# Normed, transposed and split input rows kept in DRAM between two projections of a hybrid encoder layer

## The chip, the cores and the metric

The kernel runs on one core of a Trainium2 chip. The metric is device time in microseconds for one execution of the whole program, both request batches included. The core has five engines with a queue each: PE (TensorE, matrix products), DVE (VectorE), ACT (ScalarE), POOL (GpSimd) and SP (SyncE, which here issues most of the transfers). Each engine works through its queue in order and waits on semaphores. Transfers issued from SP, ACT or POOL are carried out by 16 DMA engines.

## The reference

One encoder layer is applied to two inputs with the same weights: a sample of 2048 tokens and a prompt of 512, both 1024 wide. All is float32.

```python
h = rms_norm(x, norm1_g)
p = h @ w_in                                  # 1024 -> 1792 columns
q, k, v = p[..., :512], p[..., 512:640], p[..., 640:768]
pool_in, hy_in = p[..., 768:1024], p[..., 1024:]
a = windowed_attention(q, k, v, ...)          # blocks of 128, QK norm, ALiBi, sink
b = multiscale_pool(pool_in, ...)
c = hyena_mixer(hy_in, ..., filters, ...)     # FFT convolutions, two orders
cat = concat(rms_norm(a), rms_norm(b), rms_norm(c))
x = x + cat @ w_out
h = rms_norm(x, norm2_g)
u = dwconv3(h @ w_ffn_in)                     # 1024 -> 2 * 2816 columns
x = x + (gelu(u[..., :2816]) * u[..., 2816:]) @ w_ffn_out
```

## The kernel before, in words

**Products.** A float32 product is made of three faster ones: each operand is split into a high part, which is a rounded copy written by ScalarE, and a low part, the difference, written by VectorE. `mm3` (L326, L327, L328) issues high x high, high x low and low x high into one PSUM bank. So each operand lives on the chip as a pair, twice its size.

**Input rows.** For a block of 128 tokens ("a row" below) `norm_load` (L338) loads 512 KB into the tile `nx`, which has two buffers. `norm` squares and sums it (ACT, L346), forms the mean (DVE, L347) and the inverse root (POOL, L349, tile `rr`) and scales it (DVE, L350). `norm_t` then transposes it in eight pieces of 128x128 on PE (L360), four to a bank, and splits each bank into the tile `h`: high part by ACT (L363), low part by DVE (L364). The result of a row is 128 partitions x 2 parts x 8 pieces x 128 tokens, 1 MB.

**The front.** `front` makes the first projection of both inputs. The combined matrix is too large to stay in SBUF as split pairs, so the columns are taken in two passes over the rows of the sample, and two over the prompt. The list `rows` holds this order: 16 rows of the sample for the columns of pooling and hyena (kind `p`, result transposed, `project_p`, stored to `pT`), then 16 rows of the sample and 4 of the prompt for query, key and value (kind `q`, `project_qkv`, stored to `qkv`), then the 4 rows of the prompt for the columns of kind `p`. Before the change each of these 40 entries goes through `norm_load`, `norm` and `norm_t`. Rows of kind `p` come in pairs into tiles `h0` and `h1` of 256 tokens; rows of kind `q` alternate between two halves of one tile `h0`. Weight blocks of 256 columns are loaded as `raw` (four loads of 256 KB, two buffers) and split into `W0` to `W3` (ACT L320, DVE L321). After the projections `front` makes the output product of the sample (L1240, stored to `x2`), which needs the attention.

**What sets the order.** `front` is the main generator, and a second chain (`side` in `run`) does the filter spectra, pooling, hyena, attention, and the start of the feed-forward part. `drive` steps one and the other by counts of nominal cost. `feed` is a background generator of `front`: it prepares row `i` as soon as `blocked(i)` allows, that is when the buffer's last reader has been issued; `xs` holds two normed rows ahead, with a nominal time before which their transposes are not issued. From these steps a scheduling layer forms a static order for every engine, so a change of the steps also changes where other work stands.

**The queues around the change.** SP issues, among others, `nx`, `raw`, the spectra's loads `dec` (L721) and `tf` (L755), the hyena's loads, and the stores of the projections (`pTs` L488, `qkvs` L511). POOL issues the stores of `x2` (L651) and computes `rr`, pooling sums and the key and query norms of the attention (`hr` L1016, `kn` L1057, `qn` L1062).

Of the kernel before, what the change touches and what calls it, by code (L numbers as in the profile page):

```python
# [11 lines left out]
F32 = mybir.dt.float32  # L12
# [7 lines left out]
KD = DM // 128  # L20
# [12 lines left out]
class Seq:  # L33


    def __init__(self, name, L):
        self.name = name
        self.L = L
        self.N2 = 2 * L // 64
        self.J = self.N2 // 2  # L40
        self.R = self.N2 // 4
        self.G = 32 // self.J
        self.Cp = 256 // self.G
        self.NC = self.Cp // 64
        self.NB = L // 128
# [197 lines left out]
class Trunk:  # L243
    def __init__(self, ctx, tc, d):
        self.ctx, self.tc, self.nc, self.d = ctx, tc, tc.nc, d
        self.dr = ctx.enter_context(tc.tile_pool(name="dr", bufs=1, space=DRAM, reuse_waits="tile"))
        self.qkv, self.pT, self.kd, self.cat, self.x2, self.act = {}, {}, {}, {}, {}, {}
        for s in SEQS.values():
            n = s.name
            self.qkv[n] = self.dr.tile([s.L, 768], F32, name="qkv" + n)  # L250
            self.pT[n] = self.dr.tile([DM, s.L], F32, name="pT" + n)
            self.kd[n] = self.dr.tile([2, 128, 32, s.Cp], F32, name="kd" + n)
            self.cat[n] = self.dr.tile([DM, s.L], F32, name="cat" + n)
            self.x2[n] = self.dr.tile([s.L, DM], F32, name="x2" + n)
            self.act[n] = self.dr.tile([D_FF, s.L], F32, name="act" + n)
        self.ops = [self.dr.tile([128, 7, 4, FH], F32, name=f"ops{i}") for i in range(2)]
# [111 lines left out]
    def front(self):  # L368


        nc, tc, d = self.nc, self.tc, self.d
        S, P = SEQS["s"], SEQS["p"]
        rows = [("p", "s", t) for t in range(S.NB)] + [("q", s.name, t) for s in (S, P) for t in range(s.NB)]
        rows += [("p", "p", t) for t in range(P.NB)]
        NS, NQ, NT = S.NB, P.NB + S.NB, len(rows)
        with tc.tile_pool(name="front", bufs=1, reuse_waits="tile") as pool:
            two = ExitStack()

# [3 lines left out]
            st = {"chunks": 0, "rows": 0, "n": 0, "pace": PACE}  # L382
            widen()
            H, ready, xs, pend = {}, set(), [], []

            def load(i):
                _, n, t = rows[i]
                return self.norm_load(pool, d["x_" + n][0, t * 128:t * 128 + 128, :], 128, NXB)

            def wide(tag, here):  # L390
                return (pool if here else st["more"]).tile([128, 2, KD * 256], F32R, tag=tag, name=tag)
# [22 lines left out]
            def step():  # L414
                if pend and next(pend[0], -1) == -1:
                    pend.pop(0)

            def finish(g):
                while g in pend:
                    step()  # L420

            def norm(i, x):
                xs.append((self.norm(pool, g1, x, 128), self.now + T_NORM))

            def place(i):

                kind, n, t = rows[i]
                if kind == "p":
                    j = (i if n == "s" else i - NQ) // 2
                    if i % 2 == 0:  # L430
                        b = j % 2 if n == "s" else (j + 1) % 2
                        H[j] = wide(f"h{b}", b == 0).rearrange("p a (k f) -> p a k f", k=KD)
                    return H[j][:, 0], H[j][:, 1], i % 2 * 128
                if i == NS:
                    t = wide("h0", True)
                    st["hq"] = [t[:, i].rearrange("p (a k t) -> p a k t", a=2, k=KD) for i in range(2)]
                v = st["hq"][i % 2]
                return v[:, 0], v[:, 1], 0

            def blocked(i):  # L440
                kind, n, _ = rows[i]
                if kind == "q":
                    return st["chunks"] < NS // 2 - 1 or st["rows"] < i - NS - 1
                if n == "s":
                    return st["chunks"] < i // 2 - 1
                return "wide" not in st if (i - NQ) // 2 == NS // 2 else st["rows"] < NQ

            def feed():
                for i in range(2, NT):
                    while blocked(i):  # L450
                        yield None
                    x, t = xs.pop(0)
                    yield from self.until(t)
                    yield from self.norm_t(x, 128, *place(i), gt)
                    if i + 2 < NT:
                        norm(i + 2, load(i + 2))
                    ready.add(i)

            def also(it):

# [65 lines left out]
            norm(1, x0[1])  # L526
            for i in range(2):
                step()
                for _ in self.norm_t(xs.pop(0)[0], 128, *place(i), self.rotate((0, 1, 2))):
                    pass  # L530
                ready.add(i)
            finish(wp[0][1])
            self.strict = False
            for i in range(2, 4):
                norm(i, load(i))
            g, gt = self.rotate((0, 1)), self.rotate((2,))
            bg = feed()
            wq = []
            for j in range(NS // 2):
# [58 lines left out]
            for m in (3, 0, 1, 2):  # L598
                w, f = wp[m]
                finish(f)  # L600
                for j in js:
                    i = NQ + 2 * j
# [11 lines left out]
            t = wide("h0", True)  # L614
# [26 lines left out]
            for t in range(S.NB):  # L641
                hi, lo, sq, x, at = box.pop(0)
                yield from self.until(at)
                r = self.out_scale(pool, g, sq, GROUPS)
# [1040 lines left out]
```

## Time and profile before

| | us |
|---|---|
| median of 3 runs | 3129.38 |
| lowest, highest | 3128.49, 3129.58 |
| the profiled execution | 3122.65 |
| its span, first to last instruction | 3120.9 |

| engine | busy us | share of the span | instructions |
|---|---|---|---|
| PE | 2968.3 | 95% | 15464 |
| DVE | 1935.9 | 62% | 3138 |
| ACT | 1318.6 | 42% | 2229 |
| POOL | 595.9 | 19% | 446 |

The DMA engines moved 399.28 MB, 128 GB/s over the span. The mean granted clock of TensorE was 0.987.

How to read it: a row of instructions names the line, the engine, the operation, the tile written, an arrow and what is read, without buffer numbers; then the shape and the count, the busy time, the mean duration of one in ns, and the idle time of the engine just before these instructions with what ended most of it. A row of waits reads "who <- for whom: us in total, times, longest". PEld is the load of the stationary operand, which overlaps PE. "SPq" or "ACTq" is the queue of an engine, where transfers are issued. Since matmuls overlap in the array, a busy PE does not mean that it is at its peak.

### The profile page before, as it was taken

Reading aid. Unit: us, or ns where it says so; the run is one execution under the profiler, and the core shown is the slowest. Engines: PE = TensorE matmul, PEld = TensorE weight load, DVE = VectorE, ACT = ScalarE, POOL = GpSimd, SP = SyncE. Lnnn points to the kernel's source line nnn. Section 1 sums busy time; section 2 is a strip of 40 time slices with the busy share of each in tenths; the row PEclk is TensorE's granted clock in tenths of the full one; section 3 lists DMA queues with packets and bytes.
Section 4 is the critical chain, followed back from the end, with each engine's and each line's share of the span. In section 5 each row is a group of like instructions: output and inputs, shape, how many; then the busy total and the mean of one; then the engine's idle time right before and its main releaser. Section 6 shows DMA issues by size and latency. Waiting matters only on the chain.

```text
span 3120.9 us, 41156 instructions
## 1 busy us (share of the span) xinstructions
PE 2968.3 (95%) x15464; PEld 2464.6 (79%) x15464; DVE 1935.9 (62%) x3138; ACT 1318.6 (42%) x2229; POOL 595.9 (19%) x446
## 2 busy tenths in 40 slices
PE   7999999999999989999869999989999999999999
PEld 6887898888878867787658888868888778888887
DVE  7443567759998768766568888877777642111111
ACT  5222454448876547644344444444444431111110
POOL 1000000012333232002144444433323200000000
PEclk9999999999999999999989999989999999999999
DMA  5555586663533446576642222232222254222222
GB/s 178 146 151 143 165 233 167 188 174 99 154 97 97 145 159 200 144 201 201 215 160 70 81 81 81 81 128 82 82 81 82 76 168 134 75 81 95 75 74 75
DMA packets 433036, 399.28 MB, mean 128 GB/s; under 512 B 75641, under 2 KB 365049, under 8 KB 430021
## 3 DMA queue, kind: packets, MB, share of 16 engines
q1 hardware_dynamic: 419733, 362.14, 39.2%
q10 hardware_dynamic: 10224, 24.03, 2.0%
q0 software_dynamic: 2880, 10.49, 0.8%
q8 instruction: 122, 2.00, 0.3%
q14 instruction: 77, 0.63, 0.1%
HBM read 292.76 MB, written 103.81 MB: 127 GB/s over the span
## 4 chain that ended last, share of the span: by engine, by line
PE 44%; DMA 2%; DVE 2%; POOL 1%; issue 1%; ACT 1%; ACTq 0%; SPq 0%; POOLq 0%; DVEq 0%
PE b L326 15%; PE b L327 15%; PE b L328 15%; DMA rw<-in_w_ffn_out_dram 2%; DVE cv L1445 1%; DVE wo L321 0%; ACT wo L320 0%; POOL o L321 0%; POOL fs L1397 0%; DMA fw<-in_w_ffn_in_dram 0%; DVE cv L1450 0%; POOL fs L1399 0%; DVE o L321 0%; ACT fk L320 0%; POOL fs L1398 0%
## 5 line engine op out<-in xcount | busy, mean ns | idle before, releaser
L326 PE MATMUL b<-o,fk 128*128 128x512 f32 x1056 | 420.2, 398 | 16.9 <-ACT fk L320 13.3
L327 PE MATMUL b<-o,fk 128*128 128x512 f32 x1056 | 420.6, 398 | 5.3 <-DVE o L321 4.4
L328 PE MATMUL b<-o,fk 128*128 128x512 f32 x1056 | 420.3, 398 | 2.5 <-DVE fk L321 2.5
L326 PE MATMUL b<-wo,ah 128*128 128x512 f32 x880 | 348.9, 396 | 7.1 <-ACT wo L320 7.1
L327 PE MATMUL b<-wo,ah 128*128 128x512 f32 x880 | 348.8, 396 | 0.2 <-DVE wo L321 0.2
L328 PE MATMUL b<-wo,al 128*128 128x512 f32 x880 | 348.6, 396 | 0.1
L321 DVE TENSOR_TENSOR al<-ar,ah 128x512 fp32r<-128x512 f32 x110 | 75.9, 691 | 406.6 <-ACT ah L320 406.6
L1445 DVE SCALAR_TENSOR_TENSOR cv<-u,cst,cv 128x1024 f32<-128x1024 f32 (+2 forms) x264 | 300.7, 1180 | 7.7 <-ACT cv L1443 3.8
L320 ACT ACTIVATE ah<-ar 128x512 fp32r<-128x512 f32 x110 | 69.2, 630 | 458.1 <-PE b L327 453.1
L326 PEld LDWEIGHTS b<-o,fk 128*128 128x128 f32 x1056 | 199.9, 189 | 66.2 <-ACT fk L320 13.7
L327 PEld LDWEIGHTS b<-o,fk 128*128 128x128 f32 x1056 | 200.1, 189 | 54.5 <-DVE o L321 4.8
L328 PEld LDWEIGHTS b<-o,fk 128*128 128x128 f32 x1056 | 200.1, 189 | 52.0 <-DVE fk L321 3.7
L326 PE MATMUL b<-W,h 128*128 128x256 f32 (+1 forms) x672 | 224.7, 334 | 3.1 <-DVE x L1240 1.6
L1408 DVE TENSOR_TENSOR u<-b,u 128x512 f32<-128x512 f32 x220 | 151.2, 687 | 121.0 <-PE b L328 118.4
L327 PE MATMUL b<-W,h 128*128 128x256 f32 (+1 forms) x672 | 214.6, 319 | 0.7 <-DVE W L321 0.3
L328 PE MATMUL b<-W,h 128*128 128x256 f32 (+1 forms) x672 | 213.6, 318 | 0.0
L326 PEld LDWEIGHTS b<-wo,ah 128*128 128x128 f32 x880 | 165.5, 188 | 48.7 <-ACT wo L320 8.0
L326 PE MATMUL b<-h,W 128*128 128x256 f32 x640 | 200.6, 314 | 3.0 <-ACT W L320 1.1
L327 PEld LDWEIGHTS b<-wo,ah 128*128 128x128 f32 x880 | 165.4, 188 | 41.4 <-DVE wo L321 1.0
L328 PEld LDWEIGHTS b<-wo,al 128*128 128x128 f32 x880 | 165.5, 188 | 41.2 <-DVE al L321 0.8
L1397 POOL TENSOR_TENSOR fs<-fw 128x512 f32<-128x512 f32 x44 | 95.9, 2180 | 510.3 <-DMA fw<-in_w_ffn_in_dram 322.1
L328 PE MATMUL b<-h,W 128*128 128x256 f32 x640 | 185.3, 290 | 3.8 <-DVE W L321 3.8
(229 smaller groups left out, 6731.8 us busy)
## 6 DMA issues: line engine op xcount, KB each, us to landing
fw<-in_w_ffn_in_dram SPq DMA_DIRECT2D x132, 512.0 KB, 3.8
ar<-acts SPq DMA_DIRECT2D x88, 256.0 KB, 2.7
nx<-in_x_sample_dram SPq DMA_DIRECT2D x32, 512.0 KB, 4.5
tf<-in_t2f_s_dram SPq DMA_DIRECT2D x64, 256.0 KB, 3.2
ops<-o SPq DMA_DIRECT2D x8, 1792.0 KB, 8.7
st<-ops SPq DMA_DIRECT2D x14, 1024.0 KB, 5.4
raw<-in_w_in_dram SPq DMA_DIRECT2D x44, 256.0 KB, 3.1
acts<-cv ACTq DMA_DIRECT2D x22, 512.0 KB, 4.2
```

Source lines behind the costliest of these rows:

```text
L320: self.keep(nc.scalar.activation(hi, x, AF.Copy))
L321: self.keep((engine or nc.vector).tensor_tensor(lo, x, hi.bitcast(F32), op=ALU.subtract))
L326: nc.tensor.matmul(ps, lhsT=lhi, rhs=rhi, start=start, stop=False, skip_group_check=more)
L327: nc.tensor.matmul(ps, lhsT=lhi, rhs=rlo, start=False, stop=False, skip_group_check=more)
L328: nc.tensor.matmul(ps, lhsT=llo, rhs=rhi, start=False, stop=stop, skip_group_check=more)
L1397: nc.gpsimd.tensor_tensor(s12[:, 0:4], a21, a22, op=ALU.add)
L1408: nc.vector.tensor_tensor(o, ps, x, op=ALU.add)
L1445: nc.vector.scalar_tensor_tensor(o, u[:, part, c + i - 1:c + i - 1 + k], self.fcw[:, i, m:m + 1], o, op0=ALU.mult, op1=ALU.add)
```

## The change

Each row is normed, transposed and split once, where it is first needed. The finished pair is written to a DRAM tile `hT`, one per row of either input, and where the list comes to the row a second time, it is read back into place. `first` lists the 20 entries that are a row's first: the 16 sample rows of kind `p`, and the 4 prompt rows of kind `q`. The writes are issued on SP behind the row's split, the reads on POOL. `place` now returns one view of both parts.

```diff
@@ __init__
+            self.hT[n] = [self.dr.tile([128, 2, KD, 128], F32, name=f"hT{n}{t}") for t in range(s.NB)]
@@ front
+        first = [i for i in range(NT) if rows[i][1:] not in [r[1:] for r in rows[:i]]]
...
+            def transposed(i, x, bank):
+                v = place(i)
+                yield from self.norm_t(x, 128, v[:, 0], v[:, 1], 0, bank)
+                nc.sync.dma_start(out=self.hT[rows[i][1]][rows[i][2]], in_=v.bitcast(F32))
+                ready.add(i)
...
                 for i in range(2, NT):
                     while blocked(i):
                         yield None
+                    if i not in first:
+                        nc.gpsimd.dma_start(out=place(i), in_=self.hT[rows[i][1]][rows[i][2]])
+                        ready.add(i)
+                        continue
                     x, t = xs.pop(0)
                     yield from self.until(t)
-                    yield from self.norm_t(x, 128, *place(i), gt)
-                    if i + 2 < NT:
-                        norm(i + 2, load(i + 2))
-                    ready.add(i)
+                    yield from transposed(i, x, gt)
+                    k = first.index(i) + 2
+                    if k < len(first):
+                        norm(first[k], load(first[k]))
...
             for i in range(2):
                 step()
-                for _ in self.norm_t(xs.pop(0)[0], 128, *place(i), self.rotate((0, 1, 2))):
+                for _ in transposed(i, xs.pop(0)[0], self.rotate((0, 1, 2))):
                     pass
-                ready.add(i)
```

Over the whole program the orders differ in these counts: transposes L360 352 before, 192 after; squares L346, scalings L350 and roots L349 60 and 40 (the other 20 belong to the feed-forward part); splits L363 and L364 88 and 48 each; loads of input rows on SP 40 and 20; new are 20 writes on SP and 20 reads on POOL.

Three places. First SP at the start of the program, where the weight blocks W0 and W1 are loaded (numbers behind the names tell buffers apart). Before:

```order
L404 DMA raw_139<-in_w_in_dram 128x2x256
L338 DMA nx_163<-in_x_sample_dram 128x1024
L404 DMA raw_157<-in_w_in_dram 128x2x256
L338 DMA nx_172<-in_x_sample_dram 128x1024
L404 DMA raw_213<-in_w_in_dram 128x2x256
L721 DMA dec_636<-in_dec_s_dram 128x256
L721 DMA dec_645<-in_dec_s_dram 128x256
L755 DMA tf_883<-in_t2f_s_dram 128x512
L755 DMA tf_921<-in_t2f_s_dram 128x512
L404 DMA raw_237<-in_w_in_dram 128x2x256
```

Now (the changed file's lines: L407 is the load of `raw`, L339 that of `nx`, L445 the new write, L500 the store of `pT`):

```order
L407 DMA raw_160<-in_w_in_dram 128x2x256
L339 DMA nx_185<-in_x_sample_dram 128x1024
L445 DMA hTs0_57<-h0_144 2048x1x128
L445 DMA hTs1_58<-h0_144 2048x1x128
L407 DMA raw_179<-in_w_in_dram 128x2x256
L339 DMA nx_194<-in_x_sample_dram 128x1024
L407 DMA raw_235<-in_w_in_dram 128x2x256
L445 DMA hTs2_59<-h1_288 2048x1x128
L407 DMA raw_259<-in_w_in_dram 128x2x256
L339 DMA nx_316<-in_x_sample_dram 128x1024
L500 DMA pTs_74<-o_255 128x2x256
L407 DMA raw_263<-in_w_in_dram 128x2x256
```

The writes of rows 0 and 1 stand ahead of the fourth load of `raw`, that of row 2 ahead of the sixth, and the first loads for the spectra have moved behind the eleventh. The 128 x 2 x 8 pieces of 128 numbers (512 bytes) of a sample row are the 2048x1x128.

Second, SP later in the first projection, in the changed kernel, where the spectra's loads `dec` (L732) and `tf` (L766) and their stores `kds` (L774) pass by:

```order
L766 DMA tf_2215<-in_t2f_s_dram 128x512
L774 DMA kds_75<-ev_2024 128x4x64 x2
L445 DMA hTs10_67<-h1_2003 2048x1x128
L339 DMA nx_2051<-in_x_sample_dram 128x1024
L774 DMA kds_75<-ev_2074 128x4x64 x2
L445 DMA hTs11_68<-h1_2003 2048x1x128
L339 DMA nx_2112<-in_x_sample_dram 128x1024
L500 DMA pTs_74<-o_2142 128x2x256
L766 DMA tf_2239<-in_t2f_s_dram 128x512
```

Each write has come in between two rows of the old sequence, mostly next to the load of a later input row; the next load of `tf` stands behind it.

Third, POOL from the end of the query rows to the first attention blocks. Before:

```order
L349 TENSOR_TENSOR rr_6264<-ss_6261,mhalf_78 128x1
L349 TENSOR_TENSOR rr_6467<-ss_6464,mhalf_78 128x1
L349 TENSOR_TENSOR rr_6681<-ss_6678,mhalf_78 128x1
L1016 TENSOR_TENSOR hr_6608<-hss_6605,mhalf_78 128x5
L1057 TENSOR_TENSOR kn_6610<-kt_6598,hr_6608 128x640
```

Now (L1027, L1068 and L1073 are `hr`, `kn` and `qn`, L461 is the new read):

```order
L461 DMA h0_3131<-hTs14_71 128x2048
L461 DMA h0_3131<-hTs15_72 128x2048
L350 TENSOR_TENSOR rr_6004<-ss_6001,mhalf_98 128x1
L350 TENSOR_TENSOR rr_6248<-ss_6245,mhalf_98 128x1
L461 DMA h1_6602<-hTp0_79 128x16x128
L461 DMA h1_6602<-hTp1_80 128x16x128
L1027 TENSOR_TENSOR hr_6430<-hss_6427,mhalf_98 128x5
L1068 TENSOR_TENSOR kn_6432<-kt_6420,hr_6430 128x640
L1027 TENSOR_TENSOR hr_6439<-hss_6436,mhalf_98 128x8
L1073 TENSOR_TENSOR qn_6441<-qt_6423,hr_6439 128x1024
L461 DMA h0_7056<-hTp2_81 128x16x128
```

The sixteen reads of the sample's rows stand on POOL one behind the other (the last two are shown), where the roots `rr` stood; the prompt's four reads stand ahead of and among the attention's norms, and go to tiles of 256 tokens in pieces of 512 bytes.

More of the change, by code (lines that the diff above doesn't have):

```diff
@@ L246, in __init__ @@
         self.dr = ctx.enter_context(tc.tile_pool(name="dr", bufs=1, space=DRAM, reuse_waits="tile"))
-        self.qkv, self.pT, self.kd, self.cat, self.x2, self.act = {}, {}, {}, {}, {}, {}
+        self.qkv, self.pT, self.kd, self.cat, self.x2, self.act, self.hT = {}, {}, {}, {}, {}, {}, {}
         for s in SEQS.values():
             n = s.name
+            self.hT[n] = [self.dr.tile([128, 2, KD, 128], F32, name=f"hT{n}{t}") for t in range(s.NB)]
             self.qkv[n] = self.dr.tile([s.L, 768], F32, name="qkv" + n)
@@ L432, in place @@
                         H[j] = wide(f"h{b}", b == 0).rearrange("p a (k f) -> p a k f", k=KD)
-                    return H[j][:, 0], H[j][:, 1], i % 2 * 128
+                    return H[j][:, :, :, i % 2 * 128:i % 2 * 128 + 128]
                 if i == NS:
@@ L436, in place @@
                     st["hq"] = [t[:, i].rearrange("p (a k t) -> p a k t", a=2, k=KD) for i in range(2)]
-                v = st["hq"][i % 2]
-                return v[:, 0], v[:, 1], 0
+                return st["hq"][i % 2]
+            def transposed(i, x, bank):
[3 more added lines that the diff above has]
+                ready.add(i)
             def blocked(i):
```

## The prediction

> **What bounds the kernel now.** I read the stages first: the busy time of each engine in seven stretches (columns: stretch, its length, then busy time and instructions of PE, weight loads, DVE, ACT, POOL, the granted clock, the share of the DMA engines, GB/s).
>
> ```profile
> core 0: us, PE busy (x) PEld busy (x) DVE busy (x) ACT busy (x) POOL busy (x), PEclk, DMA share, GB/s
> 0.00:60.00 60.00, 43.38 (x249) 36.10 (x250) 40.16 (x68) 32.56 (x53) 7.57 (x12) 0.94 0.61 193
> 60.00:350.00 290.00, 280.52 (x2100) 252.31 (x2099) 134.44 (x233) 85.02 (x147) 8.77 (x16) 1.00 0.53 146
> 350.00:700.00 350.00, 325.04 (x2386) 298.64 (x2385) 235.07 (x351) 162.01 (x274) 19.39 (x22) 1.00 0.68 190
> 700.00:850.00 150.00, 138.66 (x988) 126.50 (x988) 137.71 (x374) 130.91 (x318) 46.03 (x37) 1.00 0.42 126
> 850.00:1135.00 285.00, 278.02 (x1434) 227.74 (x1433) 234.02 (x577) 173.96 (x387) 85.12 (x111) 1.00 0.37 115
> ```
>
> The first projection runs to about 350, the query rows to about 700, the prompt's second pass and the output products to 1135; spectra, hyena and attention are woven in. TensorE is busy 93 to 98% of every stretch but the start, where it works 43 of 60 us and the queues feed weights. From 700 on VectorE is nearly full too (137.71 of 150). So time leaves this kernel when PE gets fewer instructions, or waits less; VectorE's and ScalarE's savings count only through PE's waits. Nothing behind 1135 is touched, and I let it stand.
>
> A busy PE overlaps its matmuls, so I take the price of a transpose from starts, not durations. The timeline of PE around one group of four:
>
> ```profile
> 394.54 0.28 PE L326 MATMUL b<-W,h 128*128 128x256 f32 x1
> 394.66 0.28 PE L327 MATMUL b<-W,h 128*128 128x256 f32 x1
> 394.77 0.28 PE L328 MATMUL b<-W,h 128*128 128x256 f32 x1
> 394.89 0.60 PE L360 MATMUL b<-cst,nx 128*128 128x128 f32 x4
> 395.24 0.36 PE L326 MATMUL b<-W,h 128*128 128x256 f32 x1
> 395.44 0.28 PE L327 MATMUL b<-W,h 128*128 128x256 f32 x1
> ```
>
> Products follow each other every 0.12 us. From the start of the four transposes to the second product behind them 0.55 us pass, of which one product owns 0.12: four transposes displace 0.43 us.
>
> **What is removed.** Twenty of forty rows (16 query rows, 4 rows of the prompt's second pass) lose load, norm, transposes and split: 20 x 2 groups of four transposes, 40 x 0.43 = **17.2 us** of PE. The other engines, in the groups by line up to 1140 and in the waits of 350 to 700:
>
> ```profile
> L364 DVE TENSOR_TENSOR h<-b,h 128x512 fp32r<-128x512 f32 x88 | 60.0, 686 | 66.6 <-ACT h L363 66.4
> L350 DVE SCALAR_TENSOR_TENSOR nx<-nx,rr,g 128x1024 f32<-128x1024 f32 x46 | 59.3, 1288 | 23.9 <-POOL rr L349 22.6 <-DMA g<-in_norm_g_dram 1.2
> ...
> PE b L914 <- DVE zt L900: 4.7, 8, 1.2
> PE b L831 <- DVE zg L918: 3.6, 4, 1.6
> PE b L360 <- DVE h L364: 3.5, 2, 2.9
> ...
> SPq L338 <- PE b L360: 58.4, 9, 16.2
> ```
>
> PE's waits for the bank in front of a transpose go with it: **3.5 us**. VectorE loses 1.29 + 2 x 0.69 = 2.7 us a row, 43 us over the 16 query rows, 18% of its 235.07 there. The larger waits of PE for VectorE in that stretch are 4.7 and 3.6 beside a few of 1 to 2, some 13 us in all as an estimate; 18% of it is **2.5 us** (0 if they are latency, 13 if they are queueing). ScalarE loses as many instructions, without effect of its own. The last row says that SP's queue stood 58.4 us in that stretch for a buffer that the transposes free, with loads of the hyena behind it. That goes too; PE's waits for DMA there are so small that I count nothing. Gain: 17.2 + 3.5 + 2.5 = **23.2 us**.
>
> **What is added.** Twenty writes of 1 MB on SP, behind the split of each first-seen row, and twenty reads of 1 MB on POOL, against twenty loads of 512 KB that go. The nearest rows (issue, count, KB each, median us to landing):
>
> ```profile
> nx<-in_x_sample_dram SPq DMA_DIRECT2D x32, 512.0 KB, 4.5
> tf<-in_t2f_s_dram SPq DMA_DIRECT2D x64, 256.0 KB, 3.2
> ops<-o SPq DMA_DIRECT2D x8, 1792.0 KB, 8.7
> hst<-pTs SPq DMA_DIRECT2D x6, 1024.0 KB, 7.0
> x2s<-x POOLq DMA_DIRECT2D x16, 512.0 KB, 3.1
> ```
>
> `ops` is written in the same 512-byte pieces as the sample's new writes. What one write of 1 MB keeps the engines from others: at least 1.7 us for the 768 KB between `hst` and `ops`, so 2.3 for 1 MB; at most 8.7 x 1024/1792 = 5.0. In 60 to 350 a share of 0.53 moves 146 GB/s, so all engines 275, and 1 MB takes 3.8. I take 3.8, between the ends and from the stage itself.
>
> The Trainium skill, DMA: Bandwidth & Descriptors, section "Anatomy of one DMA", fits a transfer (measured on POOL's path) as about 2.0 us fixed plus bytes over 436 GB/s; by it, as an estimate, `ops` would land in 6.2 us, and the row says 8.7, so the trace does not agree for such pieces. By the page a write would occupy 2.4 us, less than the slack of 2.8 found below, and with the start at 3 the sum would be about -15 us instead of mine.
>
> *The start.* Four writes stand among the sixteen loads of the first four weight blocks. What they delay:
>
> ```profile
> 14.04 0.38 SPq L404 DMA_DIRECT2D raw<-in_w_in_dram  x1
> ...
> 14.88 0.60 ACT L363 ACTIVATE h<-b 128x512 fp32r<-128x512 f32 x1 [0.26 <-PE b L360]
> ...
> 17.80 0.61 ACT L320 ACTIVATE W<-raw 128x512 fp32r<-128x512 f32 x1
> ```
>
> The load issued at 14.04 is now behind the writes of rows 0 and 1, and the second of these waits for a split whose ScalarE half starts at 14.88. So it is issued at about 16.5 and has 2 MB ahead of it: its split comes some 7 us later than 17.80. Later blocks have two raw buffers and PE work between them, and only part comes through. I take **5 us** on PE for the whole start; ends 2 (one write's price at its lowest) and 20 (4 x 5.0).
>
> *The rest of the first projection.* Twelve writes. Behind them wait the spectra's loads, whose matmuls PE takes in order. Timelines of SP and PE:
>
> ```profile
> 196.41 0.35 SPq L755 DMA_DIRECT2D tf<-in_t2f_s_dram  x1
> ...
> 202.45 1.05 PE L758 MATMUL b<-x,tf 128*128 128x128 f32 x8
> ```
>
> From issue to use 6.0 us, landing 3.2: a slack of 2.8. A write of 3.8 ahead of such a load shows 1.0 us; between filter steps there is no such load. I take 0.4 a write, **5 us**; ends 0 and 12 x (5.0 - 2.8) = 26. The wait of a write for its split replaces a wait of the next row's load, for the transposes, at about the same place.
>
> *The query rows' reads.* POOL has nothing else in its queue there, so a waiting read holds nobody but the next. A row is 72 products of 0.12 = 8.6 us; its buffer is refilled within the row between: 7.0 landing (`hst`) and 0.6 issue leave 1 us. Later rows have hyena work between them, the first four almost none. I take **2 us**; ends 0 and 4 x (3.8 - 1.0) = 11. Over 350 to 700 the traffic grows by 8 MB, 30 us of engines at 0.68 of 350: it stays under one.
>
> The Trainium skill, same page, "Issuing engines are not separate DMA queues", says that transfers from POOL share the 16 engines with all others. The trace of before has no POOL transfer beside heavy traffic to test it on; it is why I give these reads no bandwidth of their own.
>
> *Attention.* The last reads, into two row blocks in 512-byte pieces, stand on POOL ahead of key and query norms. A POOL issue takes 0.6 us for 128 pieces:
>
> ```profile
> L651 POOL DMA_DIRECT2D x2s<-x x16: 577/610/767, 874.6 to 1136.5; - x16
> ```
>
> For 2048 pieces it lies between 0.6 and 16 times that, 39 us over four reads; POOL is busy 31% of that stretch, so at most 12 us meet waiting work. VectorE, nearly full there, loses only four rows, 11 us, so part of what PE gains earlier may queue for it. **3 us** for both; ends 0 and 12.
>
> **Sum.** -23.2 + 5 + 5 + 2 + 3 = **-8.2 us**. The profiled execution took 3122.65 (span 3120.9) and would take 3114.4; the median of the runs shown is 6.7 higher, 3129.38, and I forecast against it: **3121 us**. Every added operation hides under PE; where that cover is gone each has its upper end above.
>
> **The rivals.**
>
> *The writes pace the first projection (slower).* Each of the twelve meets the spectra's loads at the upper price: 5.0 - 2.8 = 2.2, and 0.3 for its issue, 2.5 us; 30 instead of 5 gives +16.8, **3146 us**. It decides from (23.2 - 10) / 12 = 1.1 us a write. For it: those loads run in bursts with a slack of 2.8. Against: PE's waits for them are small now, beside 512 KB row loads in the same queue. 25%.
>
> *Everything hides.* -23.2, **3106 us**: the DMA share is 0.53 and 0.68, and buffers are two deep. Against: the start, where PE already idles. 17%.
>
> *The start shows whole (no change).* Four writes at 3.8 on the weight chain, 15.2 instead of 5: +2.0, **3131 us**. For it: 43 of 60 us busy and a clock of 0.94. Against: two raw buffers. 20%.
>
> That the rows would still be made twice is excluded: the order has 192 transposes for 352.
>
> **How the numbers follow.** 38% go to the forecast, whose own range is 3114 to 3128. A run of this kernel is told from no change at about 0.2%, 6.3 us. Faster: all of "hides", four fifths of the forecast and a little of the rest, 0.49. Same: a fifth of the forecast and most of the start's rival, 0.24. Slower: the writes' rival and the start's upper part, 0.27. The range goes from 3105 to 3144: it cuts the upper part of the slower rival and any relief of VectorE beyond 2.5 us.
>
> **What would show it.** Right: 192 transposes of L360, PE's busy time down by 15 to 20 us by 1135; the waits of SP for L360 gone from the query rows; weight splits of the start 4 to 8 us later; PE's waits for `tf` grown by a few us in 60 to 350; POOL reads landing in under 8 us. Wrong: PE waiting 20 us or more for `tf`, `dec` or weight splits before 350; or a stretch from 700 to 1135 that is as long as before, with VectorE full.

## The result and the profile after

The changed kernel takes 3193.32 us, median of four runs (3192.78 to 3193.74), against 3128.94 for the kernel before beside it (3128.49 to 3129.58): a ratio of 1.0213, 95% interval 1.0200 to 1.0225. The forecast was 3121, with a range to 3144. So it is slower by 2%, and outside the range. The profiled execution has a span of 3191.0 us against 3120.9, and a mean granted clock of 0.970 against 0.987.

To see where the time went I cut both profiles at the same points of the program rather than at the same times: the first pair of rows through all four weight blocks (the fourth copy of `o`, L487 before and L499 after), the end of the first projection (the 32nd), the hyena's fifth convolution (L802, L813), the first softmax (L1117, L1128), the first output product (L1240, L1251), and the last copy into `ops` (L1331, L1342). These are the busy times in the stretches between them, before and then after (columns as in the prediction):

```profile
0.00:62.00 62.00, 45.38 (x266) 38.10 (x267) 42.06 (x72) 33.89 (x56) 7.57 (x12) 0.94 0.59 187
62.00:355.00 293.00, 283.52 (x2125) 255.31 (x2124) 133.86 (x230) 85.08 (x147) 8.77 (x16) 1.00 0.54 148
355.00:464.00 109.00, 102.17 (x757) 93.62 (x755) 71.45 (x112) 53.78 (x93) 4.53 (x6) 0.98 0.77 215
464.00:700.00 236.00, 217.87 (x1589) 200.02 (x1588) 162.30 (x239) 106.84 (x180) 14.86 (x16) 1.00 0.63 178
700.00:850.00 150.00, 138.66 (x988) 126.50 (x988) 137.71 (x374) 130.91 (x318) 46.03 (x37) 1.00 0.42 126
850.00:1539.00 689.00, 652.95 (x3287) 528.77 (x3285) 519.46 (x1116) 391.60 (x751) 153.57 (x175) 0.99 0.52 158
```

```profile
0.00:70.00 70.00, 49.77 (x261) 41.41 (x262) 44.94 (x77) 34.33 (x56) 7.36 (x12) 0.85 0.73 226
70.00:375.00 305.00, 290.50 (x2148) 260.56 (x2147) 125.62 (x219) 81.39 (x141) 8.85 (x16) 0.99 0.67 187
375.00:500.00 125.00, 106.34 (x715) 96.64 (x714) 56.27 (x90) 39.67 (x66) 3.76 (x7) 0.91 0.78 223
500.00:771.00 271.00, 239.67 (x1650) 224.23 (x1648) 145.27 (x210) 93.87 (x157) 18.88 (x19) 0.92 0.72 190
771.00:893.00 122.00, 107.31 (x716) 97.00 (x715) 104.47 (x290) 103.04 (x252) 30.08 (x23) 0.94 0.55 145
893.00:1611.00 718.00, 672.06 (x3344) 541.87 (x3343) 541.91 (x1175) 406.25 (x789) 165.66 (x185) 0.97 0.51 152
```

The first four stretches grow by 8, 12, 17 and 34 us (at the exact cuts; the rows above are cut at whole microseconds); the fifth shrinks by 28, because the projections had run ahead of the side chain, and the sixth grows by 30. Behind it the two kernels are alike. The hyena stretches (375 to 771) hold about as many PE instructions as before (2365 against 2346 in the rows above) and take longer: PE's idle time there went from 24.8 to 49.9 us (its gaps over 50 ns, summed), and the granted clock fell from 0.98 and 1.00 to 0.91 and 0.92. Before, there is one stretch of half clock between 50 and 1150; after, there are sixteen between 330 and 900.

**One loss, step by step.** The timelines of POOL, SP, ACT, DVE and PE around the hyena's switch from one job to the next, after:

```profile
590.04 0.54 POOL L461 DMA_DIRECT2D h<-hTs  x1 [28.57 <-PE b L329]
590.41 0.33 SPq L958 DMA_DIRECT2D cats<-hst  x1
598.26 0.32 SPq L809 DMA_DIRECT2D hst<-pTs  x1
603.01 2.37 ACT L813 ACTIVATE hst<-hst,mcst 128x1024 f32<-128x1024 f32 x2 [12.40 <-DMA hst<-pTs]
604.28 2.48 DVE L816 SCALAR_TENSOR_TENSOR hst<-hst,mcst 128x1024 f32<-128x1024 f32 x2 [2.09 <-ACT hst L813]
606.68 1.03 DVE L844 STREAM_TRANSPOSE hx<-b 128x512 f32<-128x512 f32 x1
607.76 2.50 PE L866 MATMUL b<-hx,tf 128*128 128x128 f32 x10 [5.10 <-DVE hx L844]
```

and the same place before:

```profile
545.98 0.33 SPq L947 DMA_DIRECT2D cats<-hst  x1
550.13 0.33 SPq L798 DMA_DIRECT2D hst<-pTs  x1
553.13 1.08 DVE L833 STREAM_TRANSPOSE hx<-b 128x512 f32<-128x512 f32 x1 [0.25 <-PE b L831]
554.98 2.38 ACT L802 ACTIVATE hst<-hst,mcst 128x1024 f32<-128x1024 f32 x2 [8.08 <-DMA hst<-pTs]
554.27 1.16 PE L855 MATMUL b<-hx,tf 128*128 128x128 f32 x8 [0.23 <-DVE hx L833]
```

A 1 MB read starts on POOL 0.37 us ahead of the 1 MB store of `hst`. The load that refills `hst` waits for that store: 4.2 us before (545.98 to 550.13), 7.9 after (590.41 to 598.26). ScalarE and VectorE follow, VectorE's transpose `hx` now stands behind the late convolution in its queue, and PE waits 5.10 us where it waited 0.23. Two causes meet here, the late store and the new order, and the run with small reads below tells them apart, since it has the new order without the large read. At the same place:

```profile
565.58 0.33 SPq L961 DMA_DIRECT2D cats<-hst  x1
569.51 0.32 SPq L812 DMA_DIRECT2D hst<-pTs  x1
579.16 1.05 PE L869 MATMUL b<-hx,tf 128*128 128x128 f32 x7 [1.34 <-DVE hx L847]
```

The load follows the store after 3.9 us, and PE waits 1.34. So of the 4.9 us by which PE's wait grew, the order alone makes 1.1 and the read the other 3.8, as far as one profile of each can say.

What this gap does to the clock is in the stretches of 3.4 us around it, after, with a second place 85 us earlier:

```profile
517.59:521.00 3.41, 1.54 (x13) 1.45 (x13) 1.91 (x2) 0.25 (x1) 0.00 (x0) 1.00 0.00 0
521.00:524.41 3.41, 3.41 (x18) 3.41 (x17) 2.10 (x4) 2.50 (x5) 0.54 (x1) 0.50 0.50 146
...
602.94:606.35 3.41, 0.00 (x0) 0.00 (x0) 2.07 (x2) 2.85 (x3) 0.00 (x0) 1.00 0.00 0
606.35:609.76 3.41, 2.00 (x9) 2.00 (x10) 3.41 (x4) 0.00 (x0) 0.00 (x0) 0.50 0.00 0
609.76:613.18 3.42, 3.42 (x18) 3.42 (x17) 1.87 (x4) 2.36 (x4) 0.00 (x0) 0.50 0.37 102
613.18:616.59 3.41, 3.41 (x32) 3.41 (x31) 2.21 (x4) 0.69 (x2) 0.54 (x1) 1.00 0.78 236
```

A busy stretch holds 32 matmuls at full clock and 18 at half. So here the gap costs its 5 us and then nearly half the work of each stretch of half clock behind it.

### The profile page after: what moved, and what is told of

The parts are those of the page before. It is cut to its first block, busy times and chain, and to the rows that moved or that the text cites. A ratio compares the mean times of both kernels' runs of the same rounds, so it can differ in the third digit from the quotient of the medians.

```text
span 3191.0 us, 40671 instructions
## 1 busy us (share of the span) xinstructions
PE 2993.8 (94%) x15304; PEld 2483.5 (78%) x15304; DVE 1890.5 (59%) x3058; ACT 1275.9 (40%) x2147; POOL 597.3 (19%) x446
## 5 line engine op out<-in xcount | busy, mean ns | idle before, releaser
L321 ACT ACTIVATE ah<-ar 128x512 fp32r<-128x512 f32 x110 | 69.3, 631 | 457.9 <-PE b L328 457.9
L327 PE MATMUL b<-W,h 128*128 128x256 f32 (+1 forms) x672 | 231.6, 345 | 5.2 <-ACT h L321 1.5
L328 PE MATMUL b<-W,h 128*128 128x256 f32 (+1 forms) x672 | 220.2, 328 | 0.8 <-DVE W L322 0.7
L329 PE MATMUL b<-W,h 128*128 128x256 f32 (+1 forms) x672 | 217.8, 324 | 0.0
```

What stands on the lines that cost most here:

```text
L321: self.keep(nc.scalar.activation(hi, x, AF.Copy))
L327: nc.tensor.matmul(ps, lhsT=lhi, rhs=rhi, start=start, stop=False, skip_group_check=more)
L328: nc.tensor.matmul(ps, lhsT=lhi, rhs=rlo, start=False, stop=False, skip_group_check=more)
L329: nc.tensor.matmul(ps, lhsT=llo, rhs=rhi, start=False, stop=stop, skip_group_check=more)
```

## The experiments

Three theories were to be told apart, beside the losses of the first projection. **Traffic**: the added megabytes make transfers late on which the hyena's chain waits. **Pacing**: a row that is read back yields no nominal steps (two of 450 were given by a transposed row), so the interleaving lets the front run ahead of the side chain. **Filler**: the transposes themselves stood between the steps of the hyena's chain and covered its waits. All differences below are to the kernel before on the same chip in the same comparison, from the ratio; the interval in brackets.

**Writes alone.** The kernel before, plus the write:

```diff
+                if i in first:
+                    nc.sync.dma_start(out=self.hT[rows[i][1]][rows[i][2]], in_=v.bitcast(F32))
```

> The kernel before, with the twenty 1 MB writes of transposed rows added on the SP queue; nothing reads them, and every row is still made twice as before. Theory W (the writes cost the start and the first projection what the changed kernel lost there, 7.8 + 11.6 us, and nothing later): 3129 + 19 = 3148 us, end of the first projection near 374 us, and the hyena stage as long as before. Theory O (those early losses come from the order in which the instructions now stand, the writes themselves are hidden): within 5 us of 3129.

Measured 3152.39 us, +28 us (+23 to +32). The writes cost by themselves 8 us in the start, 10 in the rest of the first projection, and, against theory W, some 12 more further back in its profile, 9 of them from 482 to the first output product, where the prompt's rows are written. With writes of 64 KB (next run) the same two stretches are longer by 4.5, so about half of the 9 goes with the bytes. The waits between 70 and 355 that grew, in this kernel:

```profile
DVE kt L735 <- DMA dec<-in_dec_s_dram: 13.5, 4, 8.3
ACT o L495 <- DMA pTs<-o: 7.2, 3, 4.6
PE b L327 <- ACT o L495: 2.3, 1, 2.3
```

The second is not among ScalarE's waits there before, and the first was 0.4 us up to 1100. The store of `o` explains it: `o` has one buffer, its store lands later, and PE waits behind ScalarE. The issue rows of the first projection, before and with the writes (median landing last):

```profile
pTs<-o SPq DMA_DIRECT2D x28, 256.0 KB, 2.3
```

```profile
pTs<-o SPq DMA_DIRECT2D x29, 256.0 KB, 3.9
```

**Writes of 64 KB.** The same, with a sixteenth of the bytes:

```diff
-                    nc.sync.dma_start(out=self.hT[...][...], in_=v.bitcast(F32))
+                    nc.sync.dma_start(out=self.hT[...][...][:, 0, 0:1], in_=v[:, 0, 0:1].bitcast(F32))
```

> The kernel before with twenty added writes on SP as in the run with writes alone, but of 64 KB instead of 1 MB each; every row is still made twice. With 1 MB they cost 30 us, and from the POOL queue 36. If it is the bytes: at most 8 us above the kernel before. If it is what a further instruction on SP does, its wait for the split and the order in which the build then places its neighbours: 20 to 32 us above it.

Measured 3125.80 us, +4 us (+1 to +7). It is the bytes, not the further instructions on SP. One limit: the build orders the neighbours of a write anew by its size, so PE's order is not quite that of the run with 1 MB.

**Writes from POOL.** As the writes alone, but on the other queue:

```diff
-                    nc.sync.dma_start(out=self.hT[...][...], in_=v.bitcast(F32))
+                    nc.gpsimd.dma_start(out=self.hT[...][...], in_=v.bitcast(F32))
```

> The kernel before with the twenty writes added, as in the run with writes alone on SP, but issued from the POOL queue; every row is still made twice. That run was 30 us above the kernel before on the same chip, 8 of them by the end of the first 512 columns and 10 more by the end of the first projection. Theory Q (SP's queue: the writes stand between the weight loads and the stores that free the output tile, and hold them up): at most 10 us above the kernel before. Theory B (bytes: 20 MB more through DMA engines that are already 0.6 to 0.8 busy there): still 22 to 32 us above it.

Measured 3159.79 us, +34 us (+29 to +40): theory Q falls. The Trainium skill, DMA: Bandwidth & Descriptors, section "Issuing engines are not separate DMA queues", says that transfers from any engine share the same DMA engines and that a second issuing engine saves only issue time; this run agrees, with 34 us against 28.

**Small reads.** The changed kernel, with the sample's query rows from the third on read in part: fourteen of the twenty reads bring 64 KB, six stay at 1 MB, and the rest of those fourteen rows is left out, so that their projections are of older data:

```diff
-                        nc.gpsimd.dma_start(out=place(i), in_=self.hT[rows[i][1]][rows[i][2]])
+                        v, src = place(i), self.hT[rows[i][1]][rows[i][2]]
+                        if NS + 2 <= i < NS + NQ:
+                            v, src = v[:, 0, 0:1], src[:, 0, 0:1]
+                        nc.gpsimd.dma_start(out=v, in_=src)
```

> The changed kernel, with the read-back of query rows 3 to 20 of the twenty cut from 1 MB to 64 KB each; the rest of the tile keeps the row that stood there, so the projections of those rows are of other data (this part of the computation is left out). Every instruction stays, in the same order on PE, ACT, DVE and SP. Theory T (traffic: the 1 MB reads delay the transfers that the hyena steps and the filters wait for): the 51 us lost in the stage of the query rows come back for the most part, about 3193 - 45 = 3148 us, and the clock there is near 0.99. Theory F (the order: with the transposes and their pauses gone, fewer independent matmuls stand between the steps of the hyena chain): 3188 to 3195 us, and the stage keeps some 50 us of PE idle and a clock near 0.92.

Measured 3149.57 us, +25 us (+19 to +31), against +64 for the changed kernel in a later comparison on one chip. The two hyena stretches went from 125.7 and 270.2 us to 110.5 and 245.0, as theory T has it, though the clock there came back to 0.95 and 0.99 only. The order on PE, ACT, DVE and SP is the same in both, so this is the bytes of the reads. The loads of the hyena, from the first projection's end to the first softmax, before, changed, and with small reads:

```profile
ka<-kds SPq DMA_DIRECT2D x64, 128.0 KB, 3.5
kb<-kds SPq DMA_DIRECT2D x64, 128.0 KB, 4.2
```

```profile
h<-hTs POOLq DMA_DIRECT2D x14, 1024.0 KB, 7.4
ka<-kds SPq DMA_DIRECT2D x64, 128.0 KB, 5.1
kb<-kds SPq DMA_DIRECT2D x64, 128.0 KB, 6.1
```

```profile
ka<-kds SPq DMA_DIRECT2D x64, 128.0 KB, 3.6
kb<-kds SPq DMA_DIRECT2D x64, 128.0 KB, 4.5
```

The waits say who passes it on. In that stretch, before and then in the changed kernel:

```profile
DVE t L860 <- DMA ka<-kds: 8.6, 7, 1.7
PE b L868 <- DVE t L862: 1.7, 4, 0.8
```

```profile
DVE t L871 <- ACT usw L869: 69.2, 21, 8.9
DVE t L871 <- DMA ka<-kds: 25.3, 7, 7.4
PE b L879 <- DVE t L873: 14.0, 10, 4.2
```

VectorE's product `t` waited 8.6 us for `ka` before, 25.3 now, and PE's inverse step 1.7 us for VectorE before, 14.0 now.

**Steps put back.** The changed kernel, with the pacing of the kernel before:

```diff
                         ready.add(i)
+                        yield 450
+                        yield 450
                         continue
```

> The changed kernel, with the two nominal steps of 450 that a transposed row used to give to the interleaving put back after each read-back; the reads, the writes and the removed transposes stay as they are. Theory P (pacing: front now runs ahead of the hyena work because its rows count for less): some 40 of the 51 us of the query stage come back, about 3150 us. Theory T (traffic) and theory F (missing filler matmuls): 3185 to 3198 us.

Measured 3159.12 us, +36 us (+30 to +43): 28 less than the changed kernel. Most of it as theory P says, though in other places than expected: the second hyena stretch falls from 270.2 to 247.2 us, the stretch of the output products from 718.6 to 690.2, while the fifth grows back by 22.

**Steps left out, nothing kept.** The kernel before, with the nominal steps of rows made a second time dropped:

```diff
-                    yield from self.norm_t(x, 128, *place(i), gt)
+                    for c in self.norm_t(x, 128, *place(i), gt):
+                        if i < NS or NS + S.NB <= i < NS + NQ:
+                            yield c
```

> The kernel before, every row still normed and transposed twice and nothing kept, but the nominal steps of 450 of the rows made a second time are not counted in the interleaving, as in the changed kernel. Theory P (pacing): the loss of the query stage shows without any traffic, 3160 to 3180 us. Theory T (traffic) and theory F (missing filler matmuls): within 8 us of 3129.

Measured 3144.89 us, +22 us (+15 to +28), without a byte of traffic: pacing costs by itself, less than expected. Its stretches tell how. The first softmax comes 25 us later than before (724.9 against 699.7), the last query row's copy 3 us earlier (741.1 against 744.5). By the first output product the two are level (848.5 and 849.9), but the side chain is behind, and what is left of it is woven into the output products, which take 714 us instead of 689:

```profile
848.00:1562.00 714.00, 666.39 (x3336) 535.92 (x3336) 538.19 (x1171) 406.75 (x790) 162.89 (x184) 0.98 0.51 153
```

**Steps counted double.** As a control in the other direction:

```diff
+                    for c in self.norm_t(x, 128, *place(i), gt):
+                        yield c if i < NS or NS + S.NB <= i < NS + NQ else 2 * c
```

> The kernel before, with the nominal steps of the rows made a second time counted double, 900 in place of 450; counted as nothing, they had made it 21 us slower. If the interleaving sits at an optimum: 3 to 20 us above the kernel before. If the query stage simply wants more hyena work per row: 5 to 15 us below it.

Measured 3155.50 us, +32 us (+27 to +37), more than was expected even of an optimum. The kernel before stands at a balance of the two chains that costs 20 to 30 us when it is left by 900 nominal units a row on either side. Whether any other change of the order of that size would cost as much was not tried: PE's order differs from that before at 5191 and 5159 of 15464 places in these two runs, and at 807 in the run with writes of 64 KB, which cost 4 us.

**No writes, small reads, steps put back.** What the removed work is worth. The two steps of 450 stand as above, nothing is kept, and the reads come from a weight matrix, so the projections are of other data. Fourteen reads are of 64 KB; the first two and the prompt's four stay at 1 MB:

```diff
-                nc.sync.dma_start(out=self.hT[rows[i][1]][rows[i][2]], in_=v.bitcast(F32))
...
+                        v = place(i)
+                        src = d["w_ffn_in"][0, 0:128, 0:2048].rearrange("p (a k t) -> p a k t", a=2, k=KD)
+                        if NS + 2 <= i < NS + NQ:
+                            v, src = v[:, 0, 0:1], src[:, 0, 0:1]
+                        nc.gpsimd.dma_start(out=v, in_=src)
```

> What the removed work is worth alone: the changed kernel without its writes, with the query rows after the second read as 64 KB (the tiles are filled from a weight matrix, so the projections are of other data), and with the two nominal steps of 450 per read-back row put back. If the three losses seen so far (writes 30, pacing 22, read traffic 41) are all there is, and the 160 transposes with their waits are worth the 23 us of the prediction: 23 us below the kernel before. If the transposes were filler between the steps of the hyena chain, whose absence opens new gaps: within 10 us of the kernel before.

Measured 3112.37 us, -12 us (-17 to -7): half of the 23 that the prediction had. It lies between the two expectations. The hyena's two stretches save 3 and 6 us, the output products lose 3. PE is idle for 151.8 us in all, against 148.5, and loses 47.8 to half clock, against 41.0. So of the work taken off PE some 10 us come back as waits and clock. Theory F would have it so, but the six reads that stayed large may have a share, and no run is without them; how the 10 us divide stays open.

**The same with full reads.**

```diff
-                        if NS + 2 <= i < NS + NQ:
-                            v, src = v[:, 0, 0:1], src[:, 0, 0:1]
```

> The run without writes and with the nominal steps put back, which was 11 us below the kernel before with reads of 64 KB, now with all reads of 1 MB (from a weight matrix, so the projections are of other data); the order on PE, ACT, DVE and SP is the same in both. If the bytes of the reads cost by themselves what they cost in the changed kernel: 25 to 41 us more than that run, 14 to 30 us above the kernel before. If they only cost there because the hyena work was already behind: at most 10 us more than that run, at or below the kernel before.

Measured 3138.66 us, +18 us (+11 to +24), so 30 us more than with small reads, for fourteen reads made large, with the same order on PE, ACT, DVE and SP and no writes. The reads cost by themselves. Here PE waits for the loads directly, where the run with small reads has 3.1 us of such waits; from the end of the first projection to the first softmax:

```profile
PE b L869 <- DMA tf<-in_t2f_s_dram: 14.5, 7, 5.0
```

**Reads in four pieces on SP.** The changed kernel, with

```diff
-                        nc.gpsimd.dma_start(out=place(i), in_=self.hT[rows[i][1]][rows[i][2]])
+                        v, src = place(i), self.hT[rows[i][1]][rows[i][2]]
+                        for a, k in itertools.product(range(2), range(0, KD, 4)):
+                            nc.sync.dma_start(out=v[:, a, k:k + 4].bitcast(F32), in_=src[:, a, k:k + 4])
+                            yield None
+                            yield None
```

> The changed kernel, with each 1 MB read-back issued as four 256 KB transfers on the SP queue, spread over the main line's steps, in line with the loads of the hyena work, in place of one transfer on the POOL queue. Reading 64 KB in place of 1 MB had given back 41 us of the query stage. If the burst on a second queue is what holds up the hyena loads: 25 to 40 us below the changed kernel, 70 - 33 = about 37 us above the kernel before. If the bytes alone do it, or SP's queue gets blocked instead (each piece waits there for the buffer's last matmul, with the hyena loads behind it): 60 us or more above the kernel before.

Measured 3154.93 us, +32 us (+27 to +37): half of the loss given back. But the empty steps change the interleaving too: the output products took 697.2 us instead of 718.6, which is pacing's mark. So a further run had the steps alone:

```diff
                         nc.gpsimd.dma_start(out=place(i), in_=self.hT[rows[i][1]][rows[i][2]])
+                        for _ in range(8):
+                            yield None
```

> The changed kernel with its single 1 MB reads on the POOL queue, and eight empty steps of the feeding generator after each, as the run with four pieces on SP had them; nothing else is changed. If that run's gain of 33 us over the changed kernel came from the burst being broken up on SP: 60 to 70 us above the kernel before, as the changed kernel. If it came from the steps, which change the interleaving: 28 to 42 us above the kernel before.

Measured 3177.59 us, +52 us (+46 to +59): between the two. The steps are worth some 12 of the 32 us given back, the pieces on SP some 20. They did not bring the landing back: with the pieces, `ka` still landed at a median of 5.1 us and `kb` at 5.5. How the 20 divide between the queue, the size of a piece and the order that the build then finds was not tried.

**Two combinations.** The first four rows made twice (no writes in the start), reads in pieces on SP, steps put back; writes from POOL in the first, from SP in the second:

```diff
-        first = [i for i in range(NT) if rows[i][1:] not in [r[1:] for r in rows[:i]]]
+        first = [i for i in range(NT) if rows[i][1:] not in [r[1:] for r in rows[:i]] or (rows[i][1] == "s" and rows[i][2] < 4)]
+        kept = [i for i in first if rows[i][1] == "p" or 4 <= i < NS]
...
+                if i in kept:
+                    nc.gpsimd.dma_start(out=self.hT[rows[i][1]][rows[i][2]], in_=v.bitcast(F32))
```

> A version that keeps the rows at less cost: the first four sample rows are made twice as before (no write in the start), the other sixteen are written from the POOL queue and read back as four 256 KB transfers on SP, with the two nominal steps of 450 put back. If the writes cost by SP's queue and the reads by their burst: 5 to 15 us below the kernel before. If both cost by their bytes: 25 to 45 us above it.

> The combination run before (first four sample rows made twice, reads in four pieces on SP, the two nominal steps put back), with the sixteen writes on SP in place of POOL. Writes from POOL had cost 6 us more than from SP: about 22 us above the kernel before. The removed work is worth about 11 us and sixteen writes of 1 MB at 1.5 us each cost 24, so a time below the kernel before is not expected; if it comes, the costs of writes and reads do not add.

Measured 3152.11 us, +28 us (+23 to +33), for the first, and 3138.24 us, +17 us (+12 to +22), for the second. The best of the versions that keep rows is still slower than making them twice, as the prices say: keeping a row saves 12 / 20 = 0.6 us in the run without writes and with fourteen small reads, and its write alone costs 28 / 20 = 1.4.

**The changed kernel beside them.** Unedited, for the sum:

> The changed kernel unedited, beside the others on one chip, so that the parts can be added up: 66 to 72 us above the kernel before.

Measured 3188.29 us, +64 us (+57 to +70). The parts: removed work -12 (with six large reads in it), writes +28, reads +30 (the two runs without writes), pacing +28 (changed kernel against steps put back) give +74, or +68 with pacing's own 22. So they add up within their intervals, with some overlap: with the steps put back, -12 + 28 + 30 = 46 was to be expected and 36 was measured.

The stretches of twelve of the kernels side by side, in us of one profile each (the changed kernel in two), with PE's idle time (gaps over 50 ns) and the time lost to half clock (half the length of the stretches recorded at half clock) over the whole span:

| kernel | start | first projection | to 5th convolution | to first softmax | to output product | to last `ops` | idle | half clock |
|---|---|---|---|---|---|---|---|---|
| before | 61.9 | 293.2 | 108.5 | 236.0 | 150.2 | 689.0 | 148.5 | 41.0 |
| changed | 69.7 | 305.0 | 125.7 | 270.2 | 122.2 | 718.6 | 193.1 | 95.6 |
| changed, run again | 69.8 | 307.8 | 127.7 | 269.4 | 128.7 | 710.1 | 210.5 | 78.5 |
| writes alone | 69.8 | 302.9 | 109.5 | 239.6 | 155.8 | 692.5 | 162.0 | 63.1 |
| 64 KB writes | 62.5 | 292.2 | 109.8 | 239.2 | 151.5 | 692.8 | 148.1 | 51.2 |
| writes from POOL | 68.2 | 312.5 | 107.9 | 244.6 | 158.5 | 689.0 | 168.0 | 73.4 |
| small reads | 70.0 | 308.1 | 110.5 | 245.0 | 120.8 | 713.1 | 176.5 | 64.9 |
| steps put back | 69.3 | 303.7 | 125.2 | 247.2 | 144.7 | 690.2 | 181.1 | 64.9 |
| steps left out | 60.5 | 293.2 | 118.5 | 252.6 | 123.6 | 713.6 | 161.3 | 47.8 |
| steps counted double | 61.8 | 292.2 | 113.5 | 240.2 | 174.7 | 687.9 | 171.4 | 49.5 |
| no writes, small reads | 60.0 | 294.0 | 105.2 | 230.4 | 150.4 | 692.1 | 151.8 | 47.8 |
| no writes, full reads | 61.6 | 294.3 | 123.1 | 243.2 | 147.9 | 686.6 | 170.5 | 56.3 |
| second combination | 62.8 | 300.8 | 125.4 | 236.3 | 140.4 | 687.5 | 161.6 | 56.3 |

Read by columns: the start and the first projection are long where there are 1 MB writes; the third column is near 125 where reads are full, 118 with steps left out and 114 with steps doubled, and near 110 or below elsewhere; the sixth is 710 to 719 where steps are missing. The two profiles of the changed kernel differ by 17 us in idle time and by 17 the other way in half clock, with the same sum, so a difference of that size in one of the last two columns alone says little. Of the changed kernel's 70 us (first profile), idle time grows by 45 and half clock by 55. Their sum less the 70 is 30. The work taken off PE explains some 17 of it; some 10 are counted twice, since idle time inside stretches of half clock grew from 23.5 to 43.7 us and half of it stands in both columns.

## Why the prediction failed, point by point

**"Every added operation hides under PE"** failed: the traffic has a price of its own. For the query rows' reads it had 2 us with an upper end of 11; fourteen of the sixteen cost 30 by themselves. The prediction asked whether a row's own buffer is refilled in time, and that part held: POOL's reads of the sample's rows land in 7.4 us at the median, under the 8 that were named (the prompt's four, in 512-byte pieces, in 11.7), and PE waits for any of them only once, 2.8 us for one of the prompt's. What it did not ask is what a 1 MB read does to the transfers beside it. It compared the bytes with the mean share of the DMA engines (0.68 of 350 us) and found that they fit. They fit, and still `ka` landed at 5.1 instead of 3.5 us, and a store on which a reload waits at 7.9 instead of 4.2. The hyena's chain runs from a load over VectorE back to PE, with little slack, so its latencies count, not the bytes.

**The writes** were given 10 us with the start and cost 28. The start: +5 predicted, +7.8 measured, by the mechanism named. The split that began at 17.80 now begins here, 6.4 us later where some 7 were estimated:

```profile
13.24 4.02 SPq L445 DMA_DIRECT2D hTs<-h  x2
17.31 3.30 SPq L407 DMA_DIRECT2D raw<-in_w_in_dram  x1
...
24.24 0.63 ACT L321 ACTIVATE W<-raw 128x512 fp32r<-128x512 f32 x1 [0.49 <-DMA raw<-in_w_in_dram]
```

The rest of the first projection: 0.4 us a write predicted, 9.7 / 12 = 0.8 measured with the writes alone. A cost of the size that was allowed for, but not by the loads that I priced: PE's waits for `tf` were 3.3 us in the first projection before, and are 3.1 up to 375. The store of `o`, whose row was in view with 256 KB and one buffer, was left out. And the four writes of the prompt's rows, 9 us of delay between 482 and the first output product, were not priced at all; I had put 3 us there for POOL's queue and VectorE.

**The interleaving** is the term that was missing. The prediction treated the removed steps as PE work alone. They were also the count by which the two chains are dealt out, and their loss costs 22 to 28 us. That the static order follows from these counts was known; no term and no rival came of it.

**The gain** of 23.2 us did not show whole: 12 us with no writes and fourteen small reads. PE has the 160 transposes less that were counted; their price of 0.43 us a group was not measured again. The 3.5 and 2.5 us of waits that were to go with them did not go: in the hyena stretches PE's waits for the transposes' bank are 2.8 us in that run, and those for the hyena's `tf` and `hx` rose from 1.1 and 1.8 to 3.1 and 3.5. Whether the gain itself was too high, or six reads of 1 MB hide a part of it, stays open.

**The clock** had no term. In the prediction every stretch but the start stood at 1.00, so a gap of PE cost its length. In the changed kernel a gap costs more, since it can be followed by half clock: 95.6 us are lost to it over the span, against 41.0.

**The rivals.** "The writes pace the first projection" had 3146 and the right sign, but its place (waits for the spectra's loads before 350) is not where the time is: 12 of 70 us. Neither of the two signs of failure that were named came: no 20 us of waits before 350, and no full-length stretch from 700. Neither looked at the query rows between, whose resources had seemed spare. "The start shows whole" had 15 us for the start and got 8. "Everything hides" is nearest to the run without writes and with small reads: 12 us faster, not 23.

Of the other signs, the 192 transposes, the weight splits of the start 4 to 8 us later and the end of SP's waits for L360 in the query rows came as said. PE's waits for `tf` did not grow, and PE's busy time to the end of the sample's output products did not fall but rose, from 1066.6 us (at 1136) to 1086.9 (at 1195), as more of it ran at half clock. Two readings of the prediction are slightly off, without weight for the rest: PE is busy 92% from 700 to 850, not 93 at least, and 18% of 13 us are 2.3, not 2.5.

## What to carry to other kernels

Where PE is 95% busy, storing a finished operand and reading it back has to beat the price that its bytes put on the loads around it: here a row's second making was worth 0.6 us as measured, and its 1 MB cost 28 / 20 = 1.4 us to write and 30 / 14 = 2.1 to read. Before costing added traffic by the mean share of the DMA engines, look for chains that run from a load to PE without slack and ask what each transfer's landing becomes. And when work is removed from a chain that is dealt out by nominal counts, first put the counts back: that alone returned 28 us here.

## What the runs showed of the hardware

**Half clock comes from partly idle stretches.** I cut the two profiles, before and after, by the 3.41 us in which the granted clock is recorded, and took the stretches at full clock, from 14 us on. Where PE was busy for under 40%, the next stretch was at half clock in 29 of 29 cases; between 40 and 50% in 10 of 14; between 50 and 65% in 3 of 35; above in 2 of 1679. In the first 14 us it does not hold: six stretches with PE busy for under 40%, three of them wholly idle, were followed by recorded full clock. The Trainium skill, TensorE: Matmul & The Clock Gate, section "What's actually happening", has the clock halved after an idle window of some 3.4 us, and its section "Why this matters for your kernels" asks to avoid gaps over some 3 us. The windows agree in length; a whole idle one is not needed here, as the stretch from 517.59 shows with 1.54 us busy, and in the first 14 us it was not enough.

**Large reads delay small loads beside them**, while the mean share of the DMA engines is 0.72 to 0.78: `ka`'s loads of 128 KB on SP landed at 5.1 instead of 3.5 us with 1 MB reads on POOL's queue, at 3.6 with reads of 64 KB there, and at 5.1 again with the 1 MB in four pieces on SP's own queue.

**An issue can stall.** The load issued on SP right behind two writes of 1 MB took 3.30 us to issue, where it took 0.38 before. Up to the end of the first projection no issue on SP took over 1.5 us before, ten did in the changed kernel, and one did with writes of 64 KB added to the kernel before.
